# A change to the expert routing of a hybrid diffusion block: where the router's weights are loaded, where rows are modulated, which engine makes the norm's shift

## The chip, the core and the metric

One core of a Trainium2 chip runs the whole program in one launch. The metric is the time of an execution in microseconds of the device, lower is better. The core's engines are TensorE (PE in the profile, its weight loads PEld), VectorE (DVE), ScalarE (ACT), GpSimd (POOL) and SyncE (SP), which only issues transfers here. Matrix products are written to PSUM, eight banks of 128 x 512 floats; everything else lies in SBUF.

## What is computed

Two layers over 256 latent tokens (stream 0) and 256 context tokens (stream 1) of 1024 channels. Each layer has a mixer (attention and a bidirectional recurrence), a post-norm, and an expert stage. Layer 1 needs no context stream behind the mixer. The expert stage, cut to what matters:

```python
def expert_choice_ffn(u, w_router, w_gate, w_up, w_down):
    cap = CAPACITY_FACTOR * n // N_EXPERTS               # 32 of 256 tokens
    aff = softmax(u @ w_router)                          # 16 experts
    top_w, top_idx = top_k(swapaxes(aff, 1, 2), cap)     # each expert picks 32 tokens
    xs = u[top_idx]
    h = silu(xs @ w_gate) * (xs @ w_up)
    y = (h @ w_down) * top_w
    return zeros.at[top_idx].add(y)

x = post_norm(ALPHA * x + g1 * mixer(...))
u = layer_norm(x) * (1.0 + sc2) + sh2                    # the modulation
x = post_norm(ALPHA * x + g2 * expert_choice_ffn(u, ...))
```

The scale, shift and gate rows (sc2, sh2, g2 and their likes) come from products of the conditioning vectors with `w_mod`, one set for each layer and stream. Weights are float32; the experts' weights are 201 MB a layer.

## The kernel before

**Order of the work.** `front(l)` is the mixer with its output projection and post-norm, `moe(l)` the expert stage; they run as front 0, moe 0, front 1, moe 1. Instructions are written in program order with priorities. The build gives each engine its fixed order out of a simulated timeline, in which an instruction inside `tc.high_priority(offset=PRI)` counts as if it stood 100 places earlier. `in_order(chain, ins)` writes an order out by hand: each instruction of a chain follows the one before it. On the chip every engine and queue works off its own order and waits, where it must, at the head of it.

**Buffers.** The pool T holds general tiles in rotation. The tag `t2` has two buffers of 128 x 512; the branch outputs `y`, the ranking rows `wk`, the one-hot weightings and the experts' `h` take them in turn. The pool WM holds two tiles of `w_mod` and one `mrow`. Expert weights come in tiles of 1 MB (`eload`, L1011), four for each of gate, up and down, all issued by SP in one written order; their slots lie over memory that the front used before, and each load waits until the last reader of that memory is done. One slot of each layer lies over WM.

**Modulation.** `mod_steps` (L284, L294) are fillers put between the front's work: a load of `w_mod`, then products into the bank `md`. After the eighth step `mod_cols` copies the bank to `mrow` (L247), transposes it (L250) and adds the bias (L254). The last eight steps of layer 0 and the last four of layer 1 stand behind the output projection in program order.

**Norms.** `ln_stats` takes statistics on VectorE (L323, L329, L332), and GpSimd raises to the power -0.5 (L333, operand `nhalf`). `ln_affine` is the post-norm of a token tile (L365, L370), with the gate and the residual before it (L990, L991). `ln_plain` is the norm ahead of a modulation. On VectorE it is one instruction (L347); on ScalarE (`act=True`, L345) it needs the shift -mu*r, which GpSimd makes in two steps (L343, L344, operand `neg`). Tiles of 128 tokens go to the two engines in turn. At the start of layer 1, `second(0)` norms stream 0 along one written chain on VectorE, `seq`; `pows` keeps the last GpSimd step of each norm, and the splits of the first weights (L479) are ordered behind those steps by `marks`. The end of the kernel, `finish_out`, makes its shift in the same way (L1297, L1298) for one of four output quarters, which goes over ScalarE (L1305) and GpSimd (L1306, L1307); the other three run on VectorE in a written chain (L1309, L1310). Outputs leave on SP's and ScalarE's queues.

**Routing.** In `moe`, GpSimd clears `wraw` (L1032), issues the loads of the router's weights (L1034) and multiplies them by 1 + sc2 for each stream into `wr` (L1040), which lies in the tile `oT`. TensorE multiplies sh2 with the raw weights (L1044) into a bias column `bcol` (L1045). `route(s)` takes the two token tiles of a stream. Each tile is normed, transposed in two halves of four blocks (L1061), copied from PSUM (L1063, first half on ScalarE, second on VectorE) and multiplied with `wr` (L1065). The logits get the bias on VectorE (L1068), are summed over four groups (L1070), and go through the softmax (L1073, exponential on ScalarE) and a transpose (L1077, L1078). Four rounds of eight maxima mark the 32 tokens of each expert (L1082, L1083), a running sum numbers them (L1087), one-hots follow (L1102), and the `gather` (L1136) brings the chosen columns to `xs`; there `modulate` applies scale and shift as the rows leave PSUM, on ScalarE (L385) and VectorE (L383) in turn. The experts' products are L1218 (gate, up) and L1251 (down).

```python
for h in range(2):
    p = scb()
    for m in range(4):
        nc.tensor.transpose(p[:, 128 * m:128 * m + 128], pairs(xh[:, t, :], 4 * h + m), ident)
    u = te("u2")
    (nc.vector.tensor_copy if h else nc.scalar.copy)(u, p)
```

Layer 0 routes both streams, layer 1 stream 0 alone.

Of the kernel before, what the change touches and what calls it, by code (L numbers as in the profile page):

```python
# [19 lines left out]
D = 1024  # L20
# [4 lines left out]
NE = 16  # L25
# [84 lines left out]
def tile_kernel(ctx, tc, x, c, ctx_in, c_ctx, w_mod, b_mod, w_in, attn_sink, lb_fw, lb_bw, norm_g,  # L110
# [71 lines left out]
    nc.gpsimd.memset(nhalf, -0.5)  # L182
    neg = P.tile([128, 1], F32, name="neg")
    nc.gpsimd.memset(neg, -1.0)
    pt = tr()
# [21 lines left out]
    nc.vector.tensor_copy(cols, pt[:, :24])  # L207
    ng = cols[:, 16:24]

    lbc = P.tile([128, 2, HH], F32, name="lbc")  # L210
# [67 lines left out]
    def mod_steps(l, q0, ns):  # L278

        state = {}  # L280

        def load(k, md):
            w = md.tile([128, 1024], F32, name="wmod", tag="wmod", bufs=2)
            ins = nc.sync.dma_start(w, _dram(w_mod, l * D * 6 * D + k * 128 * 6 * D + 512 * q0, [[6 * D, 128], [1, 1024]]))  # L284
            if first:
                in_order(first[:], ins)
            state[k] = w

        def work(k, md):
            if k == 0:  # L290
                state["p"] = mdb()
            pm, w = state["p"], state.pop(k)
            for j in range(4):
                mm(pm[32 * j:32 * j + 32, 0:256], scol[:, k, :], w[:, 256 * j:256 * j + 256],  # L294
                   start=(k == 0), stop=(k == KT - 1))
            if k < KT - 1:
                return
            mod_cols(l, pm, md.tile([128, 256], F32, name="mrow", tag="mrow", bufs=1), q0, 1, ns)
        return [(lambda md, k=k: load(k, md), lambda md, k=k: work(k, md)) for k in range(KT)]
# [36 lines left out]
    def ln_plain(dst, src, act=False, both=False, seq=None):  # L336
# [4 lines left out]
        if act:  # L341
            m = T.tile([128, 1], F32, name="mr", tag="mr", bufs=2)
            nc.gpsimd.tensor_tensor(m, mu, r, op=ALU.mult)  # L343
            pows.append(nc.gpsimd.tensor_tensor(m, m, neg, op=ALU.mult))  # L344
            nc.scalar.activation(dst, src, AF.Identity, bias=m, scale=r)  # L345
        else:
            nc.vector.tensor_scalar(dst, src, mu, r, op0=ALU.subtract, op1=ALU.mult)  # L347
# [76 lines left out]
    def front(l, fillers, X=None, finish=None):  # L424
# [544 lines left out]
        sG.close()  # L969


        for h in range(2):
# [26 lines left out]
    def moe(l, X, M, slots):  # L999
# [29 lines left out]
        xh, xs = M["xh"], M["xs"]  # L1029
        wr = M["oT"].rearrange("p s (k e) -> p s k e", k=KT)  # L1030
        wraw = t2("wraw")[:, :KT * 32].rearrange("p (k e) -> p k e", e=32)
        nc.gpsimd.memset(wraw, 0.0)  # L1032
        for i in range(2):
            nc.gpsimd.dma_start(wraw[:, i::2, 0:NE], _dram(w_router, l * D * NE + i * NE, [[2 * NE, 128], [256 * NE, KT // 2], [1, NE]]))  # L1034

        pl = tr()
        bcol = T.tile([128, 2], F32, name="bcol", tag="bcol")
        for s in range(S):
            for h in range(2):
                nc.gpsimd.tensor_tensor(wr[:, s, 4 * h:4 * h + 4], wraw[:, 4 * h:4 * h + 4],  # L1040
                                        MT[l][:, 8 + h, :, s, None].to_broadcast([128, 4, 32]), op=ALU.mult)
            for k in range(KT):
                j = k % 4
                mm(pl[32 * j:32 * j + 32, s:s + 1], wraw[:, k], MT[l][:, 6 + k // 4, j, s:s + 1], start=(k == j), stop=(k > j))  # L1044
        nc.vector.tensor_copy(bcol[:, 0:S], pl[:, 0:S])  # L1045
        iota = cst[:, None, None, C_IOTA:C_IOTA + CAP].to_broadcast([128, 2, 4, CAP])

        def route(s):
            pb = hsb if s else tr
            pl = pb()  # L1050
            aff = T.tile([128, 2, NE], F32, name="aff", tag="aff", bufs=2)
            wk = t2("wk")[:NE, :]
            afT, wk = wk[:, 0:256], wk[:, 256:512]
            for i in range(2):
# [3 lines left out]
                for h in range(2):  # L1058
# [3 lines left out]
                    u = te("u2")  # L1062
                    (nc.vector.tensor_copy if h else nc.scalar.copy)(u, p)  # L1063
                    for m in range(4):
                        mm(pl[32 * m:32 * m + 32, 128 * i:128 * i + 128], wr[:, s, 4 * h + m], u[:, 128 * m:128 * m + 128],  # L1065
                           start=(h == 0), stop=(h == 1))
                lT = tp("lT")[:, :128]
                nc.vector.tensor_scalar(lT, pl[:, 128 * i:128 * i + 128], bcol[:, s:s + 1], None, op0=ALU.add)  # L1068
                o = pl[:, 256 + NE * i:256 + NE * i + NE]
# [79 lines left out]
        for s in range(S):  # L1149
            onehot(0, s)  # L1150
            gather(0, s)
        o4s = []

# [139 lines left out]
        def finish_out():  # L1293

            sc = [ln_scale(*v) for v in stats]
            m = T.tile([128, 1], F32, name="mr", tag="mr", bufs=2)
            nc.gpsimd.tensor_tensor(m, *sc[0], op=ALU.mult)  # L1297
            nc.gpsimd.tensor_tensor(m, m, neg, op=ALU.mult)  # L1298
            seq = []
            for t, h in ((0, 1), (0, 0), (1, 0), (1, 1)):  # L1300
                hs = slice(512 * h, 512 * h + 512)
# [22 lines left out]
    def moe_pools(l, st, S, zones, right=()):  # L1324
# [5 lines left out]
        for z, names in enumerate((right,) + zones if right else zones):  # L1330
            Z = pool(sZ, f"ZR{l}", side="right") if names is right else pool(st, f"Z{l}{z}")
            for n in names:
                if isinstance(n, int):
                    for i in range(n):

                        w = 2304 if z == 2 + (right != ()) else 2048
                        slots.append(lambda Z=Z, i=i, w=w: Z.tile([128, w], F32, name=f"w{i}", tag=f"w{i}")[:, :2048])
                elif n not in shapes:
# [71 lines left out]
```

## Time and profile before

| what | before |
|---|---|
| median of three runs | 1810.9 us (1810.57 to 1813.97) |
| profiled execution | 1812.94 us, span 1811.2 us |
| busy: TensorE, VectorE | 1562.6 us (86%), 677.1 us (37%) |
| busy: ScalarE, GpSimd | 450.0 us (25%), 305.1 us (17%) |
| HBM read | 523.23 MB, 289 GB/s over the span |
| chain that ended last | PE 53%, DMA 37%, DVE 4%, ACT 2%, POOL 2% |

The span runs from the first to the last profiled instruction of the core; the execution's own time has a little around it. Busy time is an average over stages with different limits: the expert stages and the fronts must be read by themselves. L numbers are lines of the kernel before. In a timeline's row, the brackets hold the idle time of the engine ahead of the instruction and what ended it. SPq is SP's queue of transfers, ACTq that of ScalarE. The clock column gives the TensorE clock that was granted as a share of 2.4 GHz.

### The profile page before, as it was taken

The page shows a single profiled execution, that of the slowest core. Times are in us where ns is not written, and L with a number is a line of the kernel's source. Part 1 is how long each engine was busy: PE and PEld are TensorE (multiplying, and loading weights), DVE is VectorE, ACT ScalarE, POOL GpSimd, SP SyncE. Part 2 cuts the span into 40 slices and gives each one's busy share as a digit, 9 for nine tenths or more (in the row PEclk, how much of TensorE's full clock was granted, in tenths as well). Part 3 has the DMA queues.
Part 4 walks back from the last instruction along what each step waited for, and adds up shares of the span by engine and source line. Part 5 has one row for each costly group of instructions (what it writes and reads, how often), then busy time and mean ns, then how long its engine had stood idle before and what let it go on. Part 6 is the DMA issues. An engine that isn't in the chain of part 4 may idle for free.

```text
span 1811.2 us, 27388 instructions
## 1 busy us (share of the span) xinstructions
PE 1562.6 (86%) x11342; PEld 925.0 (51%) x11342; DVE 677.1 (37%) x1430; ACT 450.0 (25%) x850; POOL 305.1 (17%) x302
## 2 busy tenths in 40 slices
PE   6999999999989999997998899998968766666666
PEld 4777776688754433332323788775845222322222
DVE  4546566323661221211213756666751100100102
ACT  2436556323120100101000533576410000000000
POOL 2342121123310000000002633331610000000001
PEclk9999999999979999999999999999979777867887
DMA  9644123533679999999999653424689999999997
GB/s 323 186 117 127 60 82 129 177 126 117 245 308 385 421 421 421 421 422 421 421 421 379 208 178 105 130 92 131 241 341 408 421 421 422 420 421 421 421 421 287
DMA packets 159436, 526.06 MB, mean 290 GB/s; under 512 B 9896, under 2 KB 94064, under 8 KB 111184
## 3 DMA queue, kind: packets, MB, share of 16 engines
q1 hardware_dynamic: 157136, 517.46, 74.1%
q0 software_dynamic: 1456, 4.49, 0.7%
q10 hardware_dynamic: 720, 2.36, 0.4%
q8 instruction: 89, 1.46, 0.3%
q14 instruction: 35, 0.29, 0.0%
HBM read 523.23 MB, written 1.05 MB: 289 GB/s over the span
## 4 chain that ended last, share of the span: by engine, by line
PE 53%; DMA 37%; DVE 4%; ACT 2%; POOL 2%; issue 1%; SPq 1%; POOLq 0%; ACTq 0%; DVEq 0%
DMA w<-in_w_up_dram 13%; DMA w<-in_w_down_dram 12%; PE acc L168 9%; DMA w<-in_w_gate_dram 9%; PE acc L170 8%; PE acc L169 8%; PE acc L1218 8%; PE o L1251 4%; DMA wmod<-in_w_mod_dram 3%; PE md L294 2%; PE sc L701 2%; PE sc L724 1%; PE o L663 1%; PE tr L719 1%; PE hs L649 1%
## 5 line engine op out<-in xcount | busy, mean ns | idle before, releaser
L1218 PE MATMUL acc<-w,xs 128*32 128x256 f32 (+1 forms) x3064 | 402.9, 512 | 92.0 <-DMA w<-in_w_up_dram 48.9
L1218 PEld LDWEIGHTS acc<-w,xs 128*32 128x32 f32 (+1 forms) x3064 | 138.0, 130 | 339.2 <-issue 175.9
L1251 PE MATMUL o<-w,hT 128*32 128x256 f32 (+1 forms) x1432 | 188.9, 507 | 44.9 <-DMA w<-in_w_down_dram 30.5
L168 PE MATMUL acc<-uTh,wh 128*128 128x512 f32 (+1 forms) x592 | 215.1, 365 | 3.0 <-ACT qr L682 1.3
L169 PE MATMUL acc<-uTl,wh 128*128 128x512 f32 (+1 forms) x592 | 212.0, 358 | 1.4 <-DVE uTl L398 1.4
L170 PE MATMUL acc<-uTh,wl 128*128 128x512 f32 (+1 forms) x592 | 210.1, 355 | 0.0
L1229 ACT ACTIVATE h<-acc 128x512 f32<-128x512 f32 (+1 forms) x32 | 15.7, 491 | 522.2 <-PE acc L1218 509.4
L479 POOL TENSOR_TENSOR wl<-win,wh 128x1024 fp32r<-128x1024 f32 x44 | 113.4, 2579 | 164.3 <-ACT wh L478 164.3
L1251 PEld LDWEIGHTS o<-w,hT 128*32 128x32 f32 (+1 forms) x1432 | 63.5, 130 | 149.0 <-issue 66.7
L1230 DVE TENSOR_TENSOR h<-h,acc 128x512 f32<-128x512 f32 (+1 forms) x32 | 17.7, 552 | 293.4 <-PE acc L1218 293.4
L168 PEld LDWEIGHTS acc<-uTh,wh 128*128 128x128 f32 x592 | 111.9, 190 | 28.0 <-issue 6.7
L169 PEld LDWEIGHTS acc<-uTl,wh 128*128 128x128 f32 x592 | 112.3, 190 | 18.3 <-issue 2.8
L170 PEld LDWEIGHTS acc<-uTh,wl 128*128 128x128 f32 x592 | 112.1, 189 | 17.6 <-issue 3.4
L478 ACT CAST wh<-win 128x1024 fp32r<-128x1024 f32 x84 | 84.0, 1047 | 88.0 <-PE acc L169 61.9
L1110 POOL TENSOR_TENSOR OW<-OH,aff 128x256 f32<-128x256 f32 x8 | 4.9, 616 | 583.9 <-PE sc L1233 569.0
L1274 DVE TENSOR_TENSOR Y<-o,g2 OH 32x512 f32<-32x512 f32 x60 | 41.2, 687 | 140.1 <-PE o L1251 139.3
L479 DVE TENSOR_TENSOR wl<-win,wh 128x1024 fp32r<-128x1024 f32 x40 | 51.7, 1294 | 84.8 <-ACT wh L478 84.6
L1235 ACT COPY hT<-sc 128x512 f32<-128x512 f32 (+1 forms) x32 | 15.3, 479 | 243.1 <-PE sc L1233 243.1
L1274 DVE TENSOR_TENSOR Y g<-o,Y g 32x256 f32<-32x256 f32 x60 | 25.2, 420 | 122.0 <-PE o L1251 121.3
L294 PE MATMUL md<-wmod,scol 128*32 128x256 f32 x640 | 59.0, 416 | 7.8 <-DMA wmod<-in_w_mod_dram 5.6
L564 DVE TENSOR_TENSOR K<-K,F 128x512 f32<-128x512 f32 x56 | 46.6, 832 | 8.9 <-PE hs L630 5.4
L333 POOL TENSOR_TENSOR mv<-mv,nhalf 128x1 f32<-128x1 f32 x26 | 24.4, 942 | 126.7 <-DVE mv L332 126.0
(450 smaller groups left out, 2373.3 us busy)
## 6 DMA issues: line engine op xcount, KB each, us to landing
w<-in_w_gate_dram SPq DMA_DIRECT2D x128, 1024.0 KB, 19.8
w<-in_w_up_dram SPq DMA_DIRECT2D x127, 1024.0 KB, 19.8
w<-in_w_down_dram SPq DMA_DIRECT2D x119, 1024.0 KB, 19.8
wmod<-in_w_mod_dram SPq DMA_DIRECT2D x80, 512.0 KB, 4.6
win<-in_w_in_dram SPq DMA_DIRECT2D x26, 1024.0 KB, 5.4
win<-in_w_in_dram SPq DMA_DIRECT2D x32, 512.0 KB, 5.3
wmod<-in_w_mod_dram SPq DMA_DIRECT2D x32, 256.0 KB, 5.9
wo<-in_w_out_dram SPq DMA_DIRECT2D x8, 1024.0 KB, 5.0
```

The source lines that it names most:

```text
L168: mm(p, a.hi, b.hi, start=start, stop=False, **kw)
L169: mm(p, a.hi, b.lo, start=False, stop=False, **kw)
L170: mm(p, a.lo, b.hi, start=False, stop=stop, **kw)
L294: mm(pm[32 * j:32 * j + 32, 0:256], scol[:, k, :], w[:, 256 * j:256 * j + 256], start=(k == 0), stop=(k == KT - 1))
L333: pows.append(nc.gpsimd.tensor_tensor(mv[:, 2:3], mv[:, 2:3], nhalf[:, 0:1], op=ALU.pow))
L478: nc.scalar.copy(hi[:, r], w[:, r])
L479: ins = eng.tensor_sub(lo[:, r], w[:, r], hi[:, r])
L564: nc.vector.tensor_tensor(kv, kv, _view(f, 0, [[nf + 1, 2], [2, nf // 2], [0, m]]), op=ALU.mult)
L701: mm(p[:, :nk], qT[:, hd // 2, tk], kT[:, 2 * g + par, k0:k0 + nk], start=True, stop=True)
L1218: ins = mm(p[MW * j:MW * j + MW, :NW], xs[:, k, e4, :], wrow(w, k)[:, NW * j:NW * j + NW], start=(k == 0), stop=(k == KT - 1))
L1251: mm(py[MW * dj:MW * dj + MW, :NW], hT[:, 128 * m + MW * j:128 * m + MW * j + MW], wrow(wd, kt)[:, NW * dj:NW * dj + NW], start=(kt == 0), ...
L1274: nc.vector.tensor_tensor(o, py[r:r + 32, :NW], g2[r:r + 32, NW * dj:NW * dj + NW], op=ALU.mult)
```

## The change

The router's weights get a tile of their own, `wrt`, cleared once at the start, and are loaded unscaled: layer 0's right after the small loads at the start of the kernel, layer 1's in layer 0's expert stage behind the first gather. The scaled copies, the bias products and `bcol` go. `route` modulates the rows as they leave PSUM, in blocks of 128 x 128 in place of 128 x 512: all on ScalarE for a stream that isn't the last of its layer, on ScalarE and VectorE in turn for the last. The logits are copied by ScalarE or VectorE accordingly, without a bias. The shift of a norm is one VectorE instruction, part of the written chain where there is one. A one-column exponential, `warm`, stands behind the branches of each front and reads the last gate's sigmoid. `mrow` moves from WM to the general tag `t2`; the slot over WM is 2048 wide like the others.

```diff
-    neg = P.tile([128, 1], F32, name="neg")
-    nc.gpsimd.memset(neg, -1.0)
+    wrt = P.tile([128, KT, 32], F32, name="wrt")
+    nc.gpsimd.memset(wrt, 0.0)
+    def router_load(l):
+        for i in range(2):
+            nc.gpsimd.dma_start(wrt[:, i::2, 0:NE], _dram(w_router, l * D * NE + i * NE, [[2 * NE, 128], [256 * NE, KT // 2], [1, NE]]))
...
     ng = cols[:, 16:24]
+    router_load(0)
...
-            mod_cols(l, pm, md.tile([128, 256], F32, name="mrow", tag="mrow", bufs=1), q0, 1, ns)
+            mod_cols(l, pm, t2("mrow")[:, :256], q0, 1, ns)
...
             m = T.tile([128, 1], F32, name="mr", tag="mr", bufs=2)
-            nc.gpsimd.tensor_tensor(m, mu, r, op=ALU.mult)
-            pows.append(nc.gpsimd.tensor_tensor(m, m, neg, op=ALU.mult))
+            ins = nc.vector.scalar_tensor_tensor(m, mu, -1.0, r, op0=ALU.mult, op1=ALU.mult)
+            if seq is not None:
+                in_order(seq, ins)
             nc.scalar.activation(dst, src, AF.Identity, bias=m, scale=r)
...
         sG.close()
+        warm = T.tile([128, 1], F32, name="warm", tag="warm", bufs=1)
+        nc.scalar.activation(warm, sgs[1, KT - 1][:, 0:1], AF.Exp)
...
-        wr = M["oT"].rearrange("p s (k e) -> p s k e", k=KT)
-        wraw = t2("wraw")[:, :KT * 32].rearrange("p (k e) -> p k e", e=32)
-        nc.gpsimd.memset(wraw, 0.0)
...
-        pl = tr()
-        bcol = T.tile([128, 2], F32, name="bcol", tag="bcol")
...
+            busy = s == S - 1
...
                     u = te("u2")
-                    (nc.vector.tensor_copy if h else nc.scalar.copy)(u, p)
                     for m in range(4):
-                        mm(pl[32 * m:32 * m + 32, 128 * i:128 * i + 128], wr[:, s, 4 * h + m], u[:, 128 * m:128 * m + 128],
+                        um = slice(128 * m, 128 * m + 128)
+                        modulate(busy and m % 2, u[:, um], p[:, um], l, 3, 4, 4 * h + m, s)
+                        mm(pl[32 * m:32 * m + 32, 128 * i:128 * i + 128], wrt[:, 4 * h + m], u[:, um],
                            start=(h == 0), stop=(h == 1))
                 lT = tp("lT")[:, :128]
-                nc.vector.tensor_scalar(lT, pl[:, 128 * i:128 * i + 128], bcol[:, s:s + 1], None, op0=ALU.add)
+                (nc.vector.tensor_copy if busy else nc.scalar.copy)(lT, pl[:, 128 * i:128 * i + 128])
...
             gather(0, s)
+        if not last:
+            router_load(l + 1)
...
             m = T.tile([128, 1], F32, name="mr", tag="mr", bufs=2)
-            nc.gpsimd.tensor_tensor(m, *sc[0], op=ALU.mult)
-            nc.gpsimd.tensor_tensor(m, m, neg, op=ALU.mult)
             seq = []
+            in_order(seq, nc.vector.scalar_tensor_tensor(m, sc[0][0], -1.0, sc[0][1], op0=ALU.mult, op1=ALU.mult))
...
-                        w = 2304 if z == 2 + (right != ()) else 2048
-                        slots.append(lambda Z=Z, i=i, w=w: Z.tile([128, w], F32, name=f"w{i}", tag=f"w{i}")[:, :2048])
+                        slots.append(lambda Z=Z, i=i: Z.tile([128, 2048], F32, name=f"w{i}", tag=f"w{i}"))
```

## Rows read from the trace of the kernel before

**Rows 1.** Windows of the one core: two stretches of layer 1, span, busy us by engine, TensorE clock, DMA share, GB/s
```profile
1350.00:1360.00 10.00, 9.48 (x110) 7.69 (x113) 2.58 (x7) 3.45 (x6) 0.00 (x0) 0.82 0.25 82
...
1400.00:1500.00 100.00, 66.97 (x692) 27.83 (x684) 13.13 (x29) 4.10 (x10) 0.62 (x1) 0.79 1.01 421
```

**Rows 2.** Waits of the loading queue, 1303 to 1362 us: total us, times, longest us
```profile
SPq L1011 <- PE acc L1218: 24.6, 5, 22.1
...
SPq L1011 <- PE md L250: 8.2, 1, 8.2
```

**Rows 3.** Timeline of GpSimd, layer 1's routing: start us, us, what, count, idle before it
```profile
1309.59 1.53 POOL L1034 DMA_DIRECT2D wraw<-in_w_router_dram  x2
...
1321.71 1.79 POOL L1040 TENSOR_TENSOR oT<-wraw,modT 128x128 f32<-128x128 f32 x2 [8.16 <-DMA wraw<-in_w_router_dram]
...
1328.66 1.90 POOL L333 TENSOR_TENSOR mv<-mv,nhalf 128x1 f32<-128x1 f32 x2 [4.63 <-DVE mv L332]
...
1330.81 1.13 POOL L344 TENSOR_TENSOR mr<-mr,neg 128x1 f32<-128x1 f32 x1
```

**Rows 4.** Timeline of VectorE, layer 1's routing
```profile
1321.96 1.28 DVE L365 SCALAR_TENSOR_TENSOR X<-X,mv,lnp 128x1024 f32<-128x1024 f32 x1
...
1324.07 1.28 DVE L370 SCALAR_TENSOR_TENSOR X<-X,mv,lnp 128x1024 f32<-128x1024 f32 x1 [0.84 <-POOL mv L333]
...
1325.28 0.69 DVE L990 TENSOR_TENSOR acc<-acc,g1b 128x512 f32<-128x512 f32 x1
...
1328.88 1.28 DVE L365 SCALAR_TENSOR_TENSOR X<-X,mv,lnp 128x1024 f32<-128x1024 f32 x1
...
1330.60 1.28 DVE L370 SCALAR_TENSOR_TENSOR X<-X,mv,lnp 128x1024 f32<-128x1024 f32 x1 [0.44 <-POOL mv L333]
...
1335.89 0.80 DVE L347 TENSOR_SCALAR xh<-X,mv 128x1024 f32<-128x1024 f32 x1
```

**Rows 5.** Timeline of ScalarE, layer 1's routing and first gather
```profile
1338.63 1.28 ACT L1073 ACT_TABLE_LOAD   x1
...
1339.93 0.27 ACT L1073 ACTIVATE aff<-tr,r 128x16 f32<-128x16 f32 x1
...
1355.09 0.46 ACT L385 ACTIVATE xs<-o,modT 128x128 f32<-128x128 f32 x1 [0.48 <-DVE xs L383]
```

**Rows 6.** Timeline of TensorE, end of layer 1's output projection and router products
```profile
1324.64 0.40 PE L170 MATMUL acc<-wh,yinl 128*128 128x512 f32 x1
...
1340.35 1.08 PE L1065 MATMUL tr<-u,oT 128*32 128x128 f32 x16 [1.31 <-ACT aff L1073]
```

**Rows 7.** Groups of ScalarE, 500 to 532 us: busy us, mean ns, idle before and releasers
```profile
L1063 ACT COPY u<-sc 128x512 f32<-128x512 f32 x4 | 2.3, 586 | 15.8 <-PE sc L1061 12.1 <-PE tr L1065 3.8
```

**Rows 8.** Timelines of VectorE and ScalarE, layer 0's routing
```profile
502.35 0.68 DVE L1063 COPY u<-sc 128x512 f32<-128x512 f32 x1
...
505.72 1.28 DVE L365 SCALAR_TENSOR_TENSOR X<-X,mv,lnp 128x1024 f32<-128x1024 f32 x1
...
513.33 0.28 ACT L1073 ACTIVATE aff<-tr,r 128x16 f32<-128x16 f32 x1 [3.88 <-DVE r L1072]
```

**Rows 9.** Timelines of VectorE and GpSimd, start of layer 1's front
```profile
993.80 0.70 DVE L360 SCALAR_TENSOR_TENSOR X<-md,mv,lnp 128x512 f32<-128x512 f32 x1
...
995.38 1.57 POOL L333 TENSOR_TENSOR mv<-mv,nhalf 128x1 f32<-128x1 f32 x1
```

**Rows 10.** Timelines of GpSimd, VectorE and ScalarE's queue at the end
```profile
1802.02 0.55 POOL L333 TENSOR_TENSOR mv<-mv,nhalf 128x1 f32<-128x1 f32 x1 [65.03 <-DVE mv L332]
...
1805.66 1.05 DVE L1310 SCALAR_TENSOR_TENSOR X<-X,mv,lnp 128x512 f32<-128x512 f32 x1
...
1807.87 0.35 ACTq L1311 DMA_DIRECT2D out_dram<-X  x1
```

**Rows 11.** DMA issues, 501.9 to 502.8 us: count, KB each, median us to landing
```profile
wmod<-in_w_mod_dram SPq DMA_DIRECT2D x2, 512.0 KB, 13.5
```

**Rows 12.** Timeline of TensorE, layer 0's routing: late modulation products
```profile
520.21 1.93 PE L294 MATMUL md<-wmod,scol 128*32 128x256 f32 x16
```

More of the change, by code (lines that the diff above doesn't have):

```diff
@@ L1029, in moe @@
         xh, xs = M["xh"], M["xs"]
-        wr = M["oT"].rearrange("p s (k e) -> p s k e", k=KT)
-        wraw = t2("wraw")[:, :KT * 32].rearrange("p (k e) -> p k e", e=32)
-        nc.gpsimd.memset(wraw, 0.0)
-        for i in range(2):
-            nc.gpsimd.dma_start(wraw[:, i::2, 0:NE], _dram(w_router, l * D * NE + i * NE, [[2 * NE, 128], [256 * NE, KT // 2], [1, NE]]))
-        pl = tr()
-        bcol = T.tile([128, 2], F32, name="bcol", tag="bcol")
[L1038 to L1045, printed above, removed]
         iota = cst[:, None, None, C_IOTA:C_IOTA + CAP].to_broadcast([128, 2, 4, CAP])
```

## The prediction

> **What bounds the kernel now.** I read the windows first, then who waits on the loading queue, then the engines one by one through both routings. The expert stage of layer 1 is bound by its loads: from 1400 to 1500 us the DMA engines are busy throughout (share 1.01, 421 GB/s), while TensorE has 67 us of work in 100 [rows 1]. They pause once just before: from 1350 to 1360 their share is 0.25, so 7.5 us are idle. The loading queue stands still for up to 22.1 us, until the first expert's products free a slot [rows 2]. So what makes the first expert start earlier closes that hole and moves the end by as much, up to 7.5 us; loads that merely arrive sooner are worth nothing. I take layer 0's expert stage to behave alike. The terms that count are then the two routings, the start of layer 1's front, and the tail. The profiled execution has a span of 1811.2 us and took 1812.94; the median of three runs is 1810.9, 2.0 below it. The sum is made inside the span and taken off the median.
>
> **Layer 1, routing.** What looks dearest is nearly free. GpSimd stands 8.16 us, up to 1321.71, for the router weights and then scales them for 1.8 us [rows 3]. But the norm's power that queues behind this had its input only when VectorE began its step at 1321.96 [rows 4]. Without the stall the power runs beside that 1.28 us step, and ends some 0.4 us after it, near 1323.7: the pair at 1328.66 ended at 1330.56, 0.4 after VectorE's step of 1328.88 [rows 3, 4]. The step of 1324.07 then starts at 1323.7. The last tile's product leaves TensorE at 1325.04 [rows 6], and VectorE took it at 1325.28 [rows 4]. So 0.2 us are won where 10 us of stall vanish.
>
> The shift is worth more. Its second GpSimd step, held for 1.13 us beside a VectorE step, ends at 1331.94 [rows 3], and ScalarE's norm waits for it. As one VectorE instruction, counted at 0.2 us, it fits the hole between 1330.16, where the step of 1328.88 ends, and 1330.60 [rows 4]. With the 0.2 above the norm starts near 1330.15, **1.8 us earlier**. If VectorE's order puts the shift behind the step of 1330.60, 0.1 is won: the low end. Tile 1's norm at 1335.89 [rows 4] followed on tile 0's work in VectorE's queue, so it moves by the same 1.8.
>
> The exponential's table load, 1.28 us from 1338.63, holds the first exponential until 1339.93 [rows 5], and TensorE's router products of tile 1 wait for that exponential until 1340.35 [rows 6]. Loaded sooner: **1.3 us**; between load and exponential lie only 0.02 us.
>
> Against this stands the split eviction. Two copies of 128x512 a tile (586 ns on ScalarE [rows 7], 0.68 us on VectorE [rows 8]) become eight modulations of 128x128. That operation in the first gather takes 0.46 us, and the engines alternate on one bank, each waiting the other out for 0.48 [rows 5]: a half takes 4 x 0.47 = 1.9 us instead of 0.6 to 0.7. Lower bound 0 (hidden under the transposes and beside the other bank's half), upper bound 1.2 for each of two tiles. I take 0.7, since each modulation follows its own transpose. The bias products and their copy go, a fraction of a microsecond off the path: 0. Sum 1.8 + 1.3 - 0.7 = **2.4 us**; ends -1.0 (0.1 + 1.3 - 2.4) and 3.1.
>
> A quarter of a copy thus costs ScalarE 78% of a whole one. The Trainium skill (Perfetto Trace Analysis, Optimizing Scalar/DVE Operations) has both sides: an overhead on every instruction, so larger operations where the engine is saturated, and smaller ones where it only keeps others waiting. By the first half, which speaks against this change, both upper bounds hold and the second rival's 1815.4 follows; by the second the sum stays. Which of them applies depends on how full ScalarE is.
>
> **Layer 0, routing.** Two of VectorE's copies lie ahead of the last tile's step at 505.72, the first at 502.35 [rows 8]; 0.68 us each, **1.4 us**, go to ScalarE, with two logits copies. The table load saved (1.28, as in [rows 5]) pays for stream 1's later evictions (0.6 a tile). Stream 0's are all on ScalarE: 16 x 0.46 = 7.4 us in place of its copies, where ScalarE idled 3.88 us ahead of 513.33 alone [rows 8]. I take +1.4; ends -3.5 (ScalarE falls behind: those 7.4 less 3.88) and +3 (the saved load counts too).
>
> **Start of layer 1's front.** The norm's chain on VectorE is written out, and the shift joins it ahead of tile 1's steps. Tile 1 began at 993.80 without waiting; now VectorE first waits for tile 0's power, which GpSimd did at 995.38, behind a weight split [rows 9]. All of tile 1's steps queue behind: 0.55 for the power, 0.2 for the shift, so 996.2, 2.4 us later. Against that GpSimd is spared the shifts, and its second split, released by the power itself, runs meanwhile and no longer delays tile 1's power. I take **-0.4**, with the row's order kept; ends -2.4 (nothing recovered) and +0.7 (power ahead of the split).
>
> **Tail.** The shift comes first in VectorE's chain there too, so the first step waits for the power (1802.02 + 0.55) and the shift. VectorE ended at 1806.71 and now ends near 1807.5. The way over ScalarE and GpSimd, which issued the last output at 1807.87, gets about 1.2 shorter [rows 10]. Last issue 1807.5 against 1807.87: **+0.4**; ends 0 and 1.2.
>
> **At nothing.** The early router load is two issues on GpSimd, 1.53 us by the pair of 1309.59 [rows 3], ahead of the modulation bias's load; other work in the start covers them, and 1.5 is the price without. Layer 1's load is issued in layer 0's expert stage, ahead of nothing on GpSimd but the one-hots' weighting; SP's queue is not touched. The table loads move among the output branches, under TensorE's products; uncovered 1.3 a layer. Modulation rows now share the two general buffers: in layer 1 the last one waits for the branch outputs and holds a PSUM bank that a gate row needs, which is used a few us later still. The loading slot that waited 8.2 us for that row's old place [rows 2] comes sooner, ahead of the same hole. Together: -3 to +0.5, taken as 0.
>
> **Sum:** 2.4 + 1.4 - 0.4 + 0.4 = 3.8 us; 1810.9 - 3.8 = **1807.1 us**, own range 1803.5 to 1809.
>
> **Rivals.** *The late modulation group holds layer 0's second ranking.* Its row tile and stream 1's ranking rows rotate through the same two buffers. Its last weights landed 13.5 us after their issue at 502 [rows 11], and its products ran at 520.21 [rows 12]; if the ranking has to follow them, layer 0 gains nothing: 1810.9 - 2.4 = 1808.5. For it: the landing; against it: TensorE could run these products from 516 on.
>
> *ScalarE becomes the bound (slower).* Stream 0's 7.4 us, a norm and the third tile's share fall into some 12 us, 501 to 513. It decides from the point where the exponential of stream 0's second tile comes later than 513.33. Then layer 0 loses 3.5 and layer 1 has its low end, -1.0, while start and tail cancel: 1815.4. For it: the price of the small operations [rows 5, 7]; against it: the idling in [rows 8].
>
> *The shift waits in VectorE's queue.* In layer 1 it lands behind the step of 1330.60 (-1.7) and the front loses its full 2.4 (-2.0): 1807.1 + 3.7 = 1810.8. For it: the order is fixed beforehand; against it: the hole in [rows 4].
>
> **Chances:** forecast 0.47, late group 0.22, shift in the queue 0.13, ScalarE 0.18. A measurement of this kernel tells 0.2%, 3.6 us, from no change. Faster: 0.42 of the forecast's 0.47, and 0.08 of the late group's, where layer 1 comes out near its good end: 0.50. Slower: the ScalarE case, 0.18. The rest, 0.32, is no change. The range holds the forecast's good end, the first three cases and the milder half of the slow one: 1803 to 1814.
>
> **What would show it.** Right: no GpSimd stall ahead of layer 1's routing, yet the step of 1324.07 only 0.4 us earlier; ScalarE's norm near 1330.2; no table load beside the exponential; the first expert's products 2.4 us earlier after the output projection, and the DMA hole shorter. Wrong: evictions back to back on ScalarE past the exponential in layer 0; VectorE idle ahead of the second ranking or of the shift; a front that has moved by more than 2 us.

## The result: 1.6% slower, and the profile after

The changed kernel takes 1840.53 us (1839.42 to 1841.08, four executions) against 1810.74 (1809.24 to 1813.97): a ratio of 1.0162, 95% interval 1.0150 to 1.0174. The forecast was 1807.1 with a range up to 1814; its sign was wrong. The profiled execution has a span of 1838.9 us, 27.7 above that of before.

The page's busy times and its chain, first of all:

```profile
PE 1582.8 (86%) x11294; PEld 930.7 (51%) x11294; DVE 690.1 (38%) x1444; ACT 459.3 (25%) x880; POOL 293.5 (16%) x278
...
PE 58%; DMA 31%; DVE 5%; ACT 3%; issue 2%; SPq 1%; POOL 0%; ACTq 0%; DVEq 0%; POOLq 0%
```

TensorE has 20.2 us more, VectorE 13.0, and GpSimd 11.6 fewer; the share of DMA in the chain fell from 37% to 31% while TensorE's rose. So the time went where TensorE leads, and not where the experts' loads do. Milestones of the two traces put a place to it (us; the output projection's end, the first expert's first product and the like are starts and ends of rows on TensorE):

| stage | before | after | difference |
|---|---|---|---|
| layer 0: front, to the end of its output projection | 500.77 | 506.09 | +5.3 |
| layer 0: routing, to the first expert's product | 33.83 | 38.84 | +5.0 |
| layer 0: experts | 439.28 | 439.26 | 0.0 |
| layer 1: last such product of layer 0 to the first projection | 30.16 | 38.48 | +8.3 |
| layer 1: rest of the front | 321.00 | 329.09 | +8.1 |
| layer 1: routing | 30.89 | 31.43 | +0.5 |
| layer 1: experts, and the tail | 430.13 + 25.14 | 430.37 + 25.34 | +0.4 |

Four places hold 26.7 of 27.7 us, and the last routing and the tail, of which the prediction spoke most, hold hardly any.

**The rows of modulation come late.** The copy of the bank `md` to `mrow`, grouped by tile (count: shortest, median, longest ns; first and last start), in the kernel before and then in the changed one (line numbers are each kernel's own):

```profile
L247 DVE COPY mrow<-md x10: 402/418/435, 115.7 to 1257.6; 128x256 f32<-128x256 f32 x10
```
```profile
L254 DVE COPY mrow<-md x10: 410/417/437, 120.8 to 1337.6; 128x256 f32<-128x256 f32 x10
```

The copies take the same time, but the last one comes 80 us later, 18.6 of them because the whole stage is later. In layer 0 the fourth moves from 325.48 to 394.60 and the fifth from 376.60 to 432.40. The timelines of VectorE and GpSimd at that fifth copy say why:

```profile
432.40 0.42 DVE L254 COPY mrow<-md 128x256 f32<-128x256 f32 x1 [2.17 <-POOL y L954]
...
431.08 1.28 POOL L954 TENSOR_TENSOR y<-y 128x512 f32<-128x512 f32 x1
```

The row waits for a branch output `y`, because both take turns in the tag `t2`, and with it waits the bank, and behind the bank the next products that TensorE was to do while it waits in the attention. Windows of these products alone, from 1100 us to the attention's end and from there to the end of the output projection (span; busy us and count of TensorE and of its weight loads; granted clock; DMA share; GB/s), before and after:

```profile
1100.00:1266.22 166.22, 13.49 (x136) 3.68 (x136) 0.98 0.38 118
1266.22:1325.04 58.82, 0.00 (x0) 0.00 (x0) 1.00 0.73 265
```
```profile
1100.00:1284.82 184.82, 9.34 (x112) 2.88 (x112) 0.96 0.35 109
1284.82:1351.76 66.94, 4.90 (x64) 1.36 (x64) 0.97 0.79 288
```

64 products that used to be done by the attention's end now lie between the projections. The stretch behind the attention is 8.1 us longer (66.94 against 58.82), which is the whole loss of that stage; 4.9 us of it are the products' own time.

**Layer 0's rankings** both follow the late group. TensorE and VectorE in the changed kernel; [rows 12] is the group before:

```profile
514.98 0.38 PE L1075 MATMUL o<-cst,aff 128*16 128x128 f32 x1
...
522.77 1.94 PE L301 MATMUL md<-wmod,scol 128*32 128x256 f32 x16
525.25 0.69 PE L257 MATMUL md<-cst,mrow 128*128 128x128 f32 x2 [0.55 <-DVE mrow L254]
525.74 0.42 PE L1075 MATMUL o<-cst,aff 128*16 128x128 f32 x1
```
```profile
517.50 0.23 DVE L1073 TENSOR_SCALAR aff<-aff,r 128x16 f32<-128x16 f32 x1
...
524.78 0.42 DVE L254 COPY mrow<-md 128x256 f32<-128x256 f32 x1 [0.80 <-PE md L301]
525.12 0.27 DVE L1076 COPY wk<-o 16x128 f32<-16x128 f32 x1
...
526.57 0.42 DVE L1080 MAX8 mx<-wk 16x8 f32<-16x256 f32 x1
```

Stream 0's last affinities are ready at 517.73 and are transposed at 525.74, behind the row of the late group; the first maxima start at 526.57, where before they started at 516.02, ahead of that row.

**The start of layer 1's front**, VectorE and then GpSimd, which answers to [rows 9]:

```profile
1007.32 2.30 DVE L350 SCALAR_TENSOR_TENSOR mr<-mv 128x1 f32<-128x1 f32 x1 [2.94 <-POOL mv L340]
1009.54 0.74 DVE L368 SCALAR_TENSOR_TENSOR X<-md,mv,lnp 128x512 f32<-128x512 f32 x1
...
1014.67 2.56 DVE L346 TENSOR_SCALAR hgT<-X,mv 128x512 f32<-128x512 f32 x1 [0.66 <-DMA wmod<-in_w_mod_dram]
1017.15 2.30 DVE L350 SCALAR_TENSOR_TENSOR mr<-mv 128x1 f32<-128x1 f32 x1
```
```profile
1004.44 2.34 POOL L487 TENSOR_TENSOR wl<-win,wh 128x1024 fp32r<-128x1024 f32 x1 [1.41 <-ACT wh L486]
1006.75 0.54 POOL L340 TENSOR_TENSOR mv<-mv,nhalf 128x1 f32<-128x1 f32 x1
1007.26 2.33 POOL L487 TENSOR_TENSOR wl<-win,wh 128x1024 fp32r<-128x1024 f32 x1
...
1014.61 4.83 POOL L487 TENSOR_TENSOR wl<-win,wh 128x1024 fp32r<-128x1024 f32 x2
```

The shift, a column of 128 x 1, takes 2.30 us, and its end stands with that of GpSimd's weight split. In layer 0's routing, with GpSimd idle, the same instruction takes 0.16 us (at 508.27). The Trainium skill (SBUF — State Buffer, Who interferes with whom) says that a VectorE instruction with two SBUF inputs and a GpSimd instruction that reads SBUF exclude each other for the whole of the one that came first; the trace agrees, 0.16 against 2.30 us.

### The profile page after: what moved, and what is told of

Read it like the earlier page. It is cut to its first block, busy times and chain, and to the rows that moved or that the text cites. A ratio compares the mean times of both kernels' runs of the same rounds, so it can differ in the third digit from the quotient of the medians.

```text
span 1838.9 us, 27307 instructions
## 1 busy us (share of the span) xinstructions
PE 1582.8 (86%) x11294; PEld 930.7 (51%) x11294; DVE 690.1 (38%) x1444; ACT 459.3 (25%) x880; POOL 293.5 (16%) x278
## 4 chain that ended last, share of the span: by engine, by line
PE 58%; DMA 31%; DVE 5%; ACT 3%; issue 2%; SPq 1%; POOL 0%; ACTq 0%; DVEq 0%; POOLq 0%
DMA w<-in_w_up_dram 11%; DMA w<-in_w_down_dram 10%; PE acc L1218 10%; PE acc L168 9%; PE acc L169 9%; PE acc L170 9%; DMA w<-in_w_gate_dram 7%; PE o L1251 5%; PE md L301 2%; PE sc L709 2%; DMA win<-in_w_in_dram 1%; PE sc L732 1%; PE tr L727 1%; DMA wmod<-in_w_mod_dram 1%; PE o L671 1%
## 5 line engine op out<-in xcount | busy, mean ns | idle before, releaser
L1251 PE MATMUL o<-w,hT 128*32 128x256 f32 (+1 forms) x1432 | 198.0, 534 | 42.1 <-DMA w<-in_w_down_dram 27.7
L572 DVE TENSOR_TENSOR K<-K,F 128x512 f32<-128x512 f32 x56 | 51.0, 911 | 11.0 <-PE hs L638 6.5
```

The lines of the kernel that those rows point to most:

```text
L572: nc.vector.tensor_tensor(kv, kv, _view(f, 0, [[nf + 1, 2], [2, nf // 2], [0, m]]), op=ALU.mult)
L1251: mm(py[MW * dj:MW * dj + MW, :NW], hT[:, 128 * m + MW * j:128 * m + MW * j + MW], wrow(wd, kt)[:, NW * dj:NW * dj + NW], start=(kt == 0), ...
```

## The experiments

Kernels named b_ start from the kernel before, those named e_ from the changed one. Ratios are to the kernel before on the same chip.

**1. The rows alone.** b_mrow is the kernel before with only this, and with the slot over WM narrowed to 2048, as in the change:

```diff
-            mod_cols(l, pm, md.tile([128, 256], F32, name="mrow", tag="mrow", bufs=1), q0, 1, ns)
+            mod_cols(l, pm, t2("mrow")[:, :256], q0, 1, ns)
```

> The kernel before with one edit: the modulation's rows are taken from the two general buffers t2 instead of their own place. Theory (buffers): each row now queues for a buffer behind the branch outputs and the rankings, so the modulation's products stop in the gap of layer 0's attention (327 to 336 us) and at 1236 us and run later beside full TensorE work, and layer 0's rankings stand behind the last row. About 5 us at the end of layer 0's front, 5 in its routing, 8 or more at the end of layer 1's front: 1826 to 1832 us, with the start and the start of layer 1's front unchanged. Rival (the rows are late only because the changed kernel's start is late): only the routing's 5 us appear, 1814 to 1817 us.

1833.86 us (1831.50 to 1835.62), ratio 1.0119 (1.0103 to 1.0134): the place of one tile costs 21.6 us. TensorE has the same 11342 instructions and is busy for 1569.4 us, 6.8 more. Its layer 1 has the mark of the changed kernel:

```profile
1280.18:1348.61 68.43, 4.91 (x64) 1.36 (x64) 0.98 0.79 282
```

The rest of layer 1's front takes 329.83 us, +8.8. Layer 0's front ends at 500.68, as before: there its copies come late too (389.89 and 428.05), but with fillers left out of the attention the first branch product behind it comes at 331.98, 4.5 us earlier than before, and the 4.4 us lost behind that product only take this back. Layer 0's routing loses 14.6, more than in the changed kernel and in another way. TensorE has the products of the late group ahead of the router's, and waits for the group's weights:

```profile
513.45 1.08 PE L294 MATMUL md<-wmod,scol 128*32 128x256 f32 x8 [9.71 <-DMA wmod<-in_w_mod_dram]
...
518.02 0.60 PE L1044 MATMUL tr<-modT,wraw 128*32 128x1 f32 x30 [0.79 <-DMA wraw<-in_w_router_dram]
```

The router weights `wraw` share `t2` with the rows here; their load is issued by GpSimd at 510.76, behind the front, and lands at 518, which adds the 0.79. That the build put the late group first because of that load is likely, but not shown. So this run shows the tag's price in layer 1; in layer 0 its price is that of an order which the changed kernel doesn't have.

**2. The shift in the written chain alone.** b_secshift takes from the change only the VectorE shift of `second(0)`.

```diff
+            if seq is not None:
+                in_order(seq, nc.vector.scalar_tensor_tensor(m, mu, -1.0, r, op0=ALU.mult, op1=ALU.mult))
```

> The kernel before with one edit: at the start of layer 1's front the norm's shift is one VectorE instruction in the written chain, everywhere else it stays on GpSimd. Theory (held shift): the shift takes about 2.3 us instead of 0.2, because a weight split runs on GpSimd beside it, and all of tile 1's norm stands behind it: the first projection of layer 1 starts 7 to 8 us later and the kernel takes 1817 to 1820 us. Rival (the prediction's size): only the wait for the power is new, 2.4 us: about 1813 us. Rival (TensorE fills the gap with modulation products): within 1 us of the kernel before.

1815.54 us (1813.66 to 1819.77), 1.0020 (1.0011 to 1.0030), +3.3. The start of layer 1's front takes 37.33 us, +7.2, with the same rows:

```profile
995.21 2.29 DVE L344 SCALAR_TENSOR_TENSOR mr<-mv 128x1 f32<-128x1 f32 x1 [1.79 <-POOL mv L333]
...
1002.56 2.56 DVE L339 TENSOR_SCALAR hgT<-X,mv 128x512 f32<-128x512 f32 x1 [0.67 <-DMA wmod<-in_w_mod_dram]
```

The rest of the front is 3.2 us shorter (317.76 against 321.00), which is no more than this stretch scatters: up to the branch products it takes 260.28 us in e_mended and 264.03 in e_halves, which are alike there. Why only 3.3 of the 7.2 us are left in the total is open.

**3. The changed kernel with that shift back on GpSimd**, e_secshift_back:

```diff
-            ins = nc.vector.scalar_tensor_tensor(m, mu, -1.0, r, op0=ALU.mult, op1=ALU.mult)
...
+                nc.gpsimd.tensor_tensor(m, mu, r, op=ALU.mult)
+                pows.append(nc.gpsimd.tensor_tensor(m, m, neg, op=ALU.mult))
```

> The changed kernel with the shift at the start of layer 1's front back on GpSimd in two steps; the shifts in the routing and at the end stay on VectorE. Theory (held shift): 7 to 8 us come back, 1832 to 1834 us, and the first projection of layer 1 starts some 10 us later than in the kernel before instead of 18.6. Rival (the late modulation rows set the end of that front whatever its start): 0 to 2 us, 1838 to 1841 us.

1829.93 us (1826.84 to 1831.97), 1.0099 (1.0078 to 1.0119). The start of layer 1's front is back at 31.14 us. Of 29.8 us, 12.1 go, where the shift alone costs 3.3. 7.3 of them are this start, and 4.9 lie in the rest of the front (324.20, against 329.09 in the changed kernel), 3.6 of these ahead of the branch products, where kernels that are alike differ by as much. So the prices of rows and shift don't simply add, and why is not shown.

**4. The router load behind the bias load.** e_start is the changed kernel with the clearing and the loads of `wrt` moved behind the load of `brow`. In the changed kernel, `brow` lands at 13.13 us, against 12.95, yet VectorE's copies of the bias stand elsewhere in its order, behind two weight splits:

```profile
22.52 1.23 DVE L487 TENSOR_TENSOR wl<-win,wh 128x1024 fp32r<-128x1024 f32 x1 [1.33 <-ACT wh L486]
26.12 1.23 DVE L487 TENSOR_TENSOR wl<-win,wh 128x1024 fp32r<-128x1024 f32 x1 [2.38 <-ACT wh L486]
27.26 0.57 DVE L247 COPY bmod<-o 128x24 f32<-128x24 f32 x6
```

Before, they start at 18.89. The first projection moves from 28.56 to 35.35.

```diff
     nc.gpsimd.dma_start(brow, _dram(b_mod, 0, [[256, 48], [1, 256]]))
+    nc.gpsimd.memset(wrt, 0.0)
+    router_load(0)
```

> The changed kernel with the clearing and the load of the router's weights written behind the load of the modulation's bias. Theory (order of the build): VectorE's copies of the bias stand ahead of the two weight splits again, as in the kernel before, the first modulations start near 23 us instead of 30, and the 5 us at the start go: 1835 to 1836 us. Rival (the start is hidden): the gap in layer 0's attention takes it up, 1840 us. Rival (the transfers themselves delay the bias): the order is back but the bias still lands late; no gain either.

1839.35 us (1833.45 to 1840.87), 1.0144 (1.0123 to 1.0165): not told apart from the changed kernel's 1.0162. The bias copies are back at 21.01, but that mends the start only in part: the projections that follow are 2.2 us later than before, in the changed kernel 5.1, and layer 0's front still ends 4.3 us later.

**5. The rows in their own place, two tries that measured something else.** e_mrow_own gives the rows their tile in WM again. The 1 KB of `wrt` no longer fits then, so the router weights, unscaled, go into `oT`, loaded just ahead of the routing; e_all_back also puts the shift back on GpSimd.

```diff
-            mod_cols(l, pm, t2("mrow")[:, :256], q0, 1, ns)
+            mod_cols(l, pm, md.tile([128, 256], F32, name="mrow", tag="mrow", bufs=1), q0, 1, ns)
...
+        wrt = M["oT"].rearrange("p s (k e) -> p (s k) e", e=32)[:, 0:KT]
```

> The changed kernel with the modulation's rows back in their own place; to make room the router's weights lie where the scaled copies lay, and are loaded ahead of the routing as in the kernel before, unscaled. Theory (buffers): the 20 us that the rows cost in the kernel before come back, and the start is in its old order: 1815 to 1820 us, with the rankings of layer 0 near 516 us; what is left is the shift at the start of layer 1's front. Rival (the modulations of 128x128 cost more than 4 us in layer 0's routing): 1821 to 1826 us. Rival (the early load was worth something): above 1826 us.

> The same kernel, and the shift at the start of layer 1's front back on GpSimd. What is left of the change: unscaled weights with the modulation as rows leave PSUM, VectorE's shift in the routings and at the end, and the table loaded sooner. Theory (the prediction's other terms hold): -2.4 in layer 1's routing, -1.4 in layer 0's and -0.4 at the tail: 1806 to 1809 us. Rival (small operations cost what they save): 1810 to 1813 us. Rival (the build orders the rest differently as well): more than 1814 us.

1830.25 us (1.0105; 1.0091 to 1.0118) and 1825.43 (1.0079; 1.0065 to 1.0092). In e_mrow_own layer 0's front ends at 499.11 and the rest of layer 1's takes 317.60 us, so the rows' price is gone from both. But `oT` comes free only at the end of the front, where the load is issued at 499.54, and layer 0's routing takes 48.5 us, 14.7 more than before. The load isn't what comes last there: it takes 6.7 us and has landed near 507. The late group stands ahead of most of the router's products again, though the rows have their own place:

```profile
509.90 1.08 PE L293 MATMUL md<-wmod,scol 128*32 128x256 f32 x8 [8.32 <-DMA wmod<-in_w_mod_dram]
```

e_all_back has the same wait of 8.32 us. The totals say nothing of the rows.

**6. The same with the load where it was before**, into `t2("wraw")`: e_rows_own. e_mended also lets the weight splits wait for the shift, in place of standing behind the power:

```diff
+        wrt = t2("wraw")[:, :KT * 32].rearrange("p (k e) -> p k e", e=32)
...
                 in_order(seq, ins)
+                pows.append(ins)
...
-                    in_order([busy[i]], ins)
+                    tc.add_manual_dep(ins.ins, busy[i].ins.name,
```

> The changed kernel with the modulation's rows back in their own place; to make room the router's unscaled weights take the general buffer that they had in the kernel before and are loaded at the same point as there, well ahead of the routing. Theory (buffers): the rankings of layer 0 stand ahead of the last modulation group again and begin near 514 to 518 us, layer 1's front ends 4 to 8 us late through the held shift alone, and the kernel takes 1812 to 1818 us. Rival (the modulations of 128x128 hold layer 0's routing): rankings begin at 520 us or later, 1819 to 1824 us.

> The same kernel, with GpSimd's second and third splits of layer 1's first weights waiting for the shift of their tile, as in the kernel that took 1810.4 us. Theory (two places undo the change, rows and held shift; the rest is worth what the prediction said): 1806 to 1809 us. Rival (the modulations of 128x128 cost 2 to 4 us in the two routings): 1809 to 1812 us, some 3 us behind the next kernel, which keeps copies of 128x512.

e_rows_own: 1814.40 us (1813.45 to 1820.80), 1.0026 (1.0013 to 1.0038). Rows in their place and no early load: 29.8 us become 3.7, the price that experiment 2 gave the shift. No modulation product is left behind the attention, and layer 0's routing takes 32.30 us. e_mended: 1811.27 us (1807.79 to 1814.18), 0.9999 (0.9990 to 1.0008); the rest of the loss is gone too. Its shift on VectorE, at the place of the 2.30 above:

```profile
995.05 0.16 DVE L342 SCALAR_TENSOR_TENSOR mr<-mv 128x1 f32<-128x1 f32 x1 [1.77 <-POOL mv L332]
```

**7. The waiting splits on the kernel before**, b_sec_sync: the edit of experiment 2 with that wait.

> The kernel before with the shift at the start of layer 1's front on VectorE, and GpSimd's second and third splits of the first weights waiting for the shift of their tile. Theory (the shift is held by the split that runs beside it): each shift takes 0.2 us instead of 2.3, the norm of tile 1 on VectorE 0.55 instead of 2.56, and the first projection of layer 1 starts near 1004 to 1006 us instead of 1010.6; 1811 to 1814 us. Rival (a shift on VectorE is slow there whatever runs on GpSimd, or the late splits cost as much): 1815 to 1818 us.

1810.40 us (1807.59 to 1812.91), 0.9991 (0.9981 to 1.0001). The start of layer 1's front takes 32.13 us in place of 37.33, with nothing changed but which engine goes first. So 5.2 of the 7.2 us are the clash. The other 2.0 have the size of the wait for tile 0's power in VectorE's queue, which stays (1.85 us idle ahead of the first shift).

**8. The small parts alone.** b_small is the kernel before with the VectorE shift in the routings and at the end, and with the early exponential.

```diff
+            if seq is None:
+                nc.vector.scalar_tensor_tensor(m, mu, -1.0, r, op0=ALU.mult, op1=ALU.mult)
...
+        nc.scalar.activation(warm, sgs[1, KT - 1][:, 0:1], AF.Exp)
```

> The kernel before with three edits: VectorE's shift in the routings, VectorE's shift at the end of the kernel, and the table loaded sooner; weights scaled as before, copies of 128x512 as before. Theory (shift and table carry the gain): -1.8 and -1.3 in layer 1's routing, -0.4 at the tail, a little in layer 0: 1806 to 1808 us. Rival (the gain hangs on the unscaled weights): 1810 to 1812 us, with the run before this one faster than it.

1808.22 us (1806.63 to 1809.38), 0.9980 (0.9971 to 0.9989): the one kernel that is clearly below the one before. ScalarE's norm comes 5.03 us behind the output projection in place of 6.93: the shift's 1.9. From that norm to the first maxima it is 12.24 us in place of 12.40: the table load brings 0.2, because the exponential now waits for VectorE, where the maximum over a token's 16 logits stands behind a copy:

```profile
1335.00 0.69 DVE L1068 COPY u<-sc 128x512 f32<-128x512 f32 x1 [1.77 <-PE sc L1066]
1335.61 0.17 DVE L1077 TENSOR_REDUCE r<-tr 128x1 f32<-128x16 f32 x1
...
1335.81 0.27 ACT L1078 ACTIVATE aff<-tr,r 128x16 f32<-128x16 f32 x1 [1.02 <-DVE r L1077]
```

These are 2.1 of the 4.1 us. The rest is not placed: other stages of the two traces differ by as much either way (start of layer 1's front +1.3, the rest of it -2.5).

**9. The small parts and the shift with waiting splits**, b_best, the edits of 7 and 8 together:

> The kernel before with VectorE's shift in the routings, at the end, and at the start of layer 1's front with the splits waiting for it, and the table loaded sooner; copies of 128x512 and scaled weights as before. Theory (the gains of the two earlier kernels, 4.1 and 2.0 us, lie in different stages and add): 1805 to 1807 us. Rival (they share a stage, or the build's order eats one): 1808 to 1810 us.

1810.54 us (1806.52 to 1816.29), 0.9998 (0.9989 to 1.0008). The gains did not add; the profiled execution, at 1807.0 of span, is among its faster ones, so its trace doesn't show why. b_small stays the best version.

**10. Each half of an eviction on one engine**, e_halves, against e_mended, where they take turns on a half:

```diff
-                        modulate(busy and m % 2, u[:, um], p[:, um], l, 3, 4, 4 * h + m, s)
+                        modulate(busy and h, u[:, um], p[:, um], l, 3, 4, 4 * h + m, s)
```

> The kernel that took 1811.3 us (rows in their own place, splits waiting for the shift) with the routing's modulations of the last stream dealt out by halves: the first four blocks on ScalarE, the other four on VectorE, so that the two engines no longer take turns on one bank. Theory (the turns cost: 1.9 us for a half against the 1.5 us that four in a row took on ScalarE in layer 0): layer 1's ranking begins 0.5 to 1.5 us earlier after the output projection than in that kernel (19.6 us there, 17.3 to 17.5 us with copies of 128x512); 1809 to 1811 us. Rival (four small operations cost the same on one engine): no earlier than 19.4 us, 1811 us or more.

1811.27 us (1806.04 to 1815.64), 0.9993 (0.9981 to 1.0005): no difference in the total, which a gain of 2 us can't show at this spread. The stage shows it: from ScalarE's norm to the first maxima 14.63 us in e_mended and 12.59 in e_halves. ScalarE in e_mended, first tile, and in e_halves:

```profile
1331.22 0.46 ACT L386 ACTIVATE u<-sc,modT 128x128 f32<-128x128 f32 x1 [1.28 <-PE sc L1057]
1332.07 0.81 ACT L386 ACTIVATE u<-sc,modT 128x128 f32<-128x128 f32 x2 [0.40 <-PE sc L1057]
1333.91 0.46 ACT L386 ACTIVATE u<-sc,modT 128x128 f32<-128x128 f32 x1 [1.02 <-DVE u L384]
```
```profile
1336.81 1.51 ACT L386 ACTIVATE u<-sc,modT 128x128 f32<-128x128 f32 x4 [1.28 <-PE sc L1057]
```

Four in a row take 1.51 us on one engine, 0.35 for each further one; in turns, each waits for the other engine, and for what stands in that engine's queue between its turns: the 1.02 us above hold VectorE's norm of tile 1 (0.81 us).

## Why the prediction was wrong

**The failed step is "At nothing".** It put the modulation rows in the two general buffers at 0, with -3 to +0.5 as ends for all of its parts, because the bank held by the last row is needed "a few us later still". That looked at one row of ten, and at the next user of its bank. b_mrow measured +21.6 us for this edit, 14.6 of them in layer 0's routing, where the changed kernel loses 5.0. What counts is what TensorE has queued behind the bank: products meant as filler for the attention's waits. They miss them and come between the projections, +8.1 us in layer 1. From the first branch product to the end of the output projection it is 65.7 to 68.5 us there in the four kernels with the rows in `t2`, and 58.4 to 58.7 in the ten with the rows in their own place.

The early router load, which "other work in the start covers", was a right reading of the queue and the wrong question. The two issues delay the bias's landing by 0.2 us, but VectorE's order was built anew, with the bias copies 8 us later. At 77 us into the span the projections are 5.07 us behind; at the first branch product behind the attention (336.67) the gap is 0.2, because fillers were left out of the attention, and at the end of the front it is 5.3 again. The last part is the rows': from that product to the end of the front the four kernels with the rows in `t2` take 168.7 to 170.4 us, the other ten 163.7 to 165.3. In b_mrow, whose start isn't late, the rows win as much in the attention as they lose behind it. So the 5.3 have the size of the late start, whose 5.07 us use up what the left-out fillers win. No run has the early load without the rows in `t2`.

**Start of layer 1's front**: predicted -0.4 with ends -2.4 and +0.7 as gain, that is a loss of 2.4 at most; measured 8.3. The sign of the low end was right, and the queue behind tile 0's power as well (2.94 us idle). Its term of 0.2 for the shift was 2.30 twice, and a 128 x 512 step of 0.55 became 2.56.

**Layer 1's routing.** The cheap stall was right: the step of 1324.07 [rows 4] is 1350.43 now, 0.36 us earlier against the output projection's end, where 0.4 was forecast. The shift was right: ScalarE's norm, which waited for the second step of [rows 3], and the exponential that answers to [rows 5]:

```profile
1356.73 1.24 ACT L353 ACTIVATE xh<-X,mr,mv 128x1024 f32<-128x1024 f32 x1 [13.19 <-DVE mr L350]
...
1366.35 0.26 ACT L1071 ACTIVATE aff<-tr,r 128x16 f32<-128x16 f32 x1
```

The norm starts 4.97 us behind that end, in place of 6.93: 1.96 won, forecast 1.8. The table load is gone from ahead of the exponential [rows 5], but was worth 0.2 and not 1.3 (b_small), since another step comes last ahead of it: VectorE's maximum in b_small, ScalarE's own modulation here. The split eviction costs 2.4 (14.63 us from the norm to the first maxima in e_mended, 12.24 in b_small with copies of 128x512), its upper bound, and not 0.7; 2.0 of it go when each half stays on one engine (e_halves). From the norm to the first maxima it is 14.88 us (1356.73 to 1371.61) in place of 12.40, so 2.48 are lost behind the norm against 1.96 won ahead of it: the stage is 0.5 longer, inside the low end of -1.0.

On the small operations the Trainium skill (Perfetto Trace Analysis, Optimizing Scalar/DVE Operations) was weighed for its overhead on every instruction. The price came out near that bound, yet e_halves has as many small operations and doesn't pay it. The turns between two engines cost, and the size by itself hardly (12.59 us in e_halves against 12.24).

**Layer 0's routing**: +1.4 forecast. With rows and load in place, e_rows_own and e_mended have 32.30 and 32.39 us against 33.83, 1.5 and 1.4. The size was right, the reason is not shown: b_best, which still has the copies of before, has 32.15, and e_halves 33.00.

**Tail**: +0.4 forecast. From the last expert's product on, kernels with the edit take 23.47 to 25.34 us and kernels without it 23.95 to 25.14, with medians of 23.7 and 24.3; from one execution of each a gain of 0.4 is neither shown nor excluded.

**The hole in the loads** didn't close; it moved with the first expert, as the forecast of what bounds the kernel would have it [rows 1]:

```profile
1377.00:1387.00 10.00, 9.46 (x106) 7.80 (x110) 2.58 (x7) 3.20 (x6) 0.00 (x0) 0.81 0.16 49
1427.63:1527.63 100.00, 70.22 (x684) 28.75 (x688) 13.13 (x29) 4.10 (x10) 0.62 (x1) 0.74 1.01 421
```

**The rivals.** The late group did hold the ranking, and both streams' rankings rather than the second. It held stream 0's by the written order, not by the late row's buffer: that ranking's first row is copied at 525.12, ahead of TensorE's reading of the late row (525.25). With rows and load undone, in e_rows_own, the first maxima come at 511.84 and the late row at 520.91; which of the two edits sets this order is not separated. The rival's time, 1808.5, counted only the gain forgone; the stage is 5.0 us longer than before. ScalarE did not become the bound: the exponential of stream 0's second tile comes at 515.85, 9.76 us behind the output projection, where before it was 12.56 [rows 8]. The shift did not wait in layer 1's routing, and in the front it was held by GpSimd's split more than by the queue. No case had the rows' price in the fronts, so the range could not hold the result.

## What to carry to other kernels

Before a tile is moved to a shared tag, list who holds that tag at each time the tile is wanted, and what stands in TensorE's queue behind the bank that the tile empties; the move of one tile cost 21.6 us here and added no operation. A small instruction moved to VectorE is priced by what GpSimd does at that moment, and where the two meet an ordering wait that lets the small one go first can give most of it back (37.33 to 32.13 us, where the kernel before has 30.16). Where the build sets the order, an edit's own cost says little of what its new order costs, so read the order of every engine after it: in three kernels here TensorE stood 8.3 to 9.7 us in layer 0's routing for weights of a group that the kernel before has behind the routing's products.

## What was not expected of the hardware

- A VectorE instruction of 128 x 1 took 0.16 us with GpSimd idle and 2.30 beside a GpSimd split of 2.33 us; one of 128 x 512 with one tile as input took 0.55 in the kernel before (at 1000.34) and 2.56 here.
- Two engines that take turns on one PSUM bank need 2.0 us more in a routing of 16 small evictions than the same number in two halves; VectorE's norm of tile 1 (0.81 us), which stands between its turns, has a part in it.
- Between executions of kernels that are alike there, the way from the first maxima to the first expert's product took 11.56 to 12.97 us. What sets this is open; it is as large as most terms of the forecast.
